# Hybrid attention and mLSTM layer on one core: a sum of weight tiles by GpSimd, a reload in halves, and later modulation items in the first FFN's up projection

## The chip, the cores and the metric

The kernel runs on one core of one Trainium2 chip. The metric is the device time of one execution, in microseconds. The comparison is by medians of several executions; a profile is one further execution, with the hardware profiler on. The engines are called PE (TensorE, matmuls), DVE (VectorE), ACT (ScalarE), POOL (GpSimd) and SP (SyncE, which here only issues transfers). PEld is TensorE's weight load, which runs beside its matmuls.

## What is computed

One layer for 256 latent and 256 context tokens of width 2048, all in fp32: a SwiGLU FFN, a token mixer (grouped attention beside a bidirectional mLSTM), a second FFN, each behind an RMSNorm with shift, scale and gate made from the condition vectors (adaLN). Cut to what the change touches:

```python
def half_step_ffn(x, mod, i, g, w_up, w_down):
    h = adaln(x, g, mod, i)
    a, b = jnp.split(h @ w_up, 2, axis=-1)
    return x + 0.5 * mod[:, i + 2, None, :] * ((jax.nn.silu(a) * b) @ w_down)

mod_l = (silu_c @ w_mod[l] + b_mod[l]).reshape(B, N_MOD, D_MODEL)      # 9 vectors of 2048
mod_c = (silu_cc @ w_mod[l] + b_mod[l]).reshape(1, N_MOD, D_MODEL)
xl = half_step_ffn(xl, mod_l, 0, g_norm[l, 0], w_ffn1_up[l], w_ffn1_down[l])
xc = half_step_ffn(xc, mod_c, 0, g_norm[l, 0], w_ffn1_up[l], w_ffn1_down[l])
hl = adaln(xl, g_norm[l, 1], mod_l, 3)                                 # the mixer: vectors 3 to 5
```

D_FF is 5632, so `w_up` is 2048 x 11264. The products `h @ w_up` are made of 128x512 matmuls in a split form: each fp32 factor is a sum hi + lo of two numbers of a shorter format, and a product is hi*hi + hi*lo + lo*hi, three matmuls (`mm3`, L124 to L126).

## The kernel before

**The stages.** The modulation vectors that the first norm needs come first; then the first FFN's up projection, its down projection, the mixer (from about 1400 us in the profile), and the second FFN (from about 2000 us). Modulation vectors 2 to 8 aren't made on PE: they are dot products on DVE that run beside the other stages as a side job.

**The up projection** takes the 44 column tiles of D_FF in 11 groups of four. The first group goes the plain way. The other ten, n = 1 to 10, are done by `quad(n)`, L660 on: a 2x2 block product with seven products in place of eight. Each quad has seven steps, and each step multiplies one form of the tokens with one form of the weights: `a11`, `a12`, `n1`, `s4`, `s2`, `s3`, `a22` (in the program's names, `hhi` holds the `a` forms and `s3`; `n1h`, `s4h`, `s2h` the others). A step has two weight tiles of 128x2048, q = 0 and 1, so a quad has 14 tiles, each with 24 matmuls of 128x512 (the two halves of the tokens, four blocks of 128 columns, three matmuls each).

**A weight tile** goes through `split` (L90): in two halves of 1024 columns, ACT writes `hi` (L102) and DVE writes `lo` = tile - hi (L103). There are four half buffers of each. PE uses the first half at once and the second six matmuls later.

**Where the tiles come from.** A quad's weights lie in memory as parts (ab, c) of 128x2048, 1 MB each. `chain_[q]` are two tiles in SBUF that hold a running sum. `raw` is a pool of three tiles. In a quad, for each q:

| step | form | tile | issued behind the tile's split |
|---|---|---|---|
| 0 | a11 | chain = part(0, q) | chain += part(1, q) |
| 1 | a12 | raw, loaded part(0, 2+q) | |
| 2 | n1 | chain | chain += part(1, 2+q) |
| 3 | s4 | `ra[q]`, loaded part(1, 2+q) | ra += part(1, q) |
| 4 | s2 | chain | chain += part(0, 2+q): a sum of four |
| 5 | s3 | `ra[q]` | |
| 6 | a22 | chain | reload: the next quad's part(0, q) (`again`, `first_chain`) |

The sums are transfers that add (`accum`, L642), issued on POOL's queue; the loads and the reload are issued by SP. An accumulating transfer waits until ACT and DVE have split the tile that it changes, and the next split of that tile waits until it has landed.

**The modulation items beside it.** `side` (from `mod_items`) does one item at a time: SP loads a 512 KB tile `sraw` (L212, two buffers), and DVE multiplies it with the conditions `cBh` and sums the row, once for each of the two sequences (`scalar_tensor_tensor`, L183). There are 96 items in the ten quads. `cBh` holds half of the conditions and is loaded twice (L178, half 0 and half 1); behind each load the items pause for `WAIT` steps (one step is one weight tile here), and the rest of the pace is a straight line that ends at step (NB - 2) * 14 + 2 = 128. The DVE instructions of the items stay in the order in which the program writes them. Each column of modulation sums that is complete is sent out by `mod_rows_out` two steps later.

`WAIT` (L34) is a global: the mixer's modulation side job (`Beside`, L304) and the second FFN's (`mod_late`, which calls `mod_items`) read it too.

**Order.** Every engine works through its instructions in a fixed order, which a scheduler sets when the program is built, from the order of the code and its own costs; instructions that are pinned (`tc.keep_in_program_order`) keep their order among each other.

Of the kernel before, what the change touches and what calls it, by code (L numbers as in the profile page):

```python
# [11 lines left out]
BF16 = mybir.dt.bfloat16  # L12
AF = mybir.ActivationFunctionType
ALU = mybir.AluOpType
# [16 lines left out]
PACE = 0.5  # L31


WAIT = 2  # L34
BLOCKS = ((0, 2), (2, 4), (4, 8), (8, 12), (12, 16))
FB = 4
CB = 512
# [11 lines left out]
def tile_layer(ctx: ExitStack, tc: tile.TileContext, I: dict, out: bass.AP):  # L49
    nc = tc.nc  # L50
# [124 lines left out]
    def conditions(cB, h0, h1, seqs=(CTX, LAT)):  # L175

        for s in seqs:
            nc.sync.dma_start(cB[s], ccd[s, h0 * 1024 : h1 * 1024].partition_broadcast(P))  # L178

    def mod_half(raw, cB, junk, i, seqs, kt, h):  # L180

        for s in seqs:
            ins = nc.vector.scalar_tensor_tensor(junk() if junk else raw, raw, 1.0, cB[s], op0=ALU.mult, op1=ALU.mult, accum_out=mT[:, i, s, kt, h : h + 1])  # L183
            tc.keep_in_program_order(ins)
# [10 lines left out]
    def mod_items(items, load, raws, n_raws, cB, junk, pace):  # L195

        waits = 0  # L200
        half = None
        done = 0
        late, ahead = [], []

        def step():

            if late and late[0][0] <= done:
                mod_rows_out(*late.pop(0)[1:])

        def fetch(i, kt, h):  # L210
            raw = raws()
            load(raw, I["w_mt"][i - 2, kt, :, h * 1024 : (h + 1) * 1024])  # L212
            ahead.append(raw)

        for item in items[:n_raws]:
            fetch(*item)
        for n, (i, kt, h) in enumerate(items):
            if cB.half(h) != half:
                half = cB.half(h)
                cB.load(half)  # L220
                waits += WAIT
            while done < np.interp(n, *zip((0, 0), *pace)) + waits:
                done += 1
                step()
                yield
            seqs = (CTX, LAT) if i < 5 else (LAT,)
            mod_half(ahead.pop(0), cB.at(h), junk, i, seqs, kt, h)
            if n + n_raws < len(items):
                fetch(*items[n + n_raws])
            left[i] -= 1  # L230
            if not left[i]:
                late += [(done + 2, i, s, v) for s, v in mod_end(i, seqs)]
        while late:
            done += 1
            step()
            yield
# [3 lines left out]
    half_items = lambda i0, i1: [(i, kt, h) for h in range(2) for i in range(i0, i1) for kt in range(KT)]  # L240
# [8 lines left out]
    class Beside:  # L249
# [46 lines left out]
        def steps(self):  # L296
            half = None
            while self.n < len(self.items) or self.due or self.late:
                while self.n < len(self.items):
                    h = self.items[self.n][2]  # L300
                    if h != half:
                        half = h
                        conditions({LAT: self.cB}, h, h + 1, (LAT,))
                        self.waits += WAIT  # L304
                    if self.done < np.interp(self.n, *zip((0, 0), *self.pace)) + self.waits:
# [13 lines left out]
    def mod_end(i, seqs):  # L319

        n, q = divmod(i, 3)
        cols = []
        for s in seqs:
            dst = (SH, SC)[q][:, n, s, :] if q < 2 else sm.tile([P, KT], F32, tag="gv", name="gv")
            mod_sum(dst, i, s, slice(0, KT))
            if q == 1:
                scale_of(n, s, slice(0, KT))
            elif q == 2:
                cols.append((s, dst))
        return cols  # L330

    def mod_rows_out(i, s, v):

        pg = tbank()
        tc.keep_in_program_order(nc.tensor.transpose(pg[:KT, :P], v, ident))
        gr = sm.tile([KT, P], F32, tag="gr", name="gr")
        nc.vector.tensor_copy(gr, pg[:KT, :P])
        nc.sync.dma_start(mod_rows[i][s, :].rearrange("(k p) -> k p", p=P), gr)
# [199 lines left out]
    with pool(name="st", bufs=1) as st:  # L538
# [16 lines left out]
        for k0, k1 in BLOCKS:  # L555
            kk = slice(k0, k1)
            n = (k1 - k0) * P
# [4 lines left out]
            for i in range(2):  # L562
                b = tbank()[:, :n]
                pm.append(b)
                for g in range(KT // nk):
# [6 lines left out]
                    for j in range(nk):  # L572
                        k = nk * g + j
                        q = 32 * (j % 4)
# [31 lines left out]
    NB = NF // FB  # L606
# [5 lines left out]
    def form(tag, name):  # L612
        sp = ft if tag == "t" else fm
        return [sp.tile([P, 2, 8, P], F32R, tag=f"{tag}{x}", name=f"{name}{x}") for x in "hl"]
# [4 lines left out]
    def pinned(ins):  # L619
        tc.keep_in_program_order(ins)  # L620
# [20 lines left out]
    chain_ = [chp.tile([P, 2048], F32, name=f"chain{c}") for c in range(2)]  # L641
    accum = lambda dst, src: nc.gpsimd.dma_start(dst, src, accum_op=ALU.add)  # L642
    with pool(name="f1u", bufs=1) as f1u:
# [14 lines left out]
        def part(n, ab, c):  # L658
            return I["w_up1b"][n - 1, ab, c]

        def first_chain(n, c):
            nc.sync.dma_start(chain_[c], part(n, 0, c))

        for c in range(2):
            first_chain(1, c)
# [13 lines left out]
        n1, s2, s4 = form("n", "n1"), form("s", "s2"), form("t", "s4")  # L679
# [66 lines left out]
        def c12_tile():  # L746
            return f1u.tile([P, CB], F32, tag="c12", name="c12", bufs=2)

        def quad(n, after=lambda step: None):

            X, Y, Z = {}, {}, {}
            ca, cy, cb, ra = {}, {}, {}, {}

            def p1(s):
                ca[s] = ca_tile()
                nc.scalar.activation(ca[s], X[s], AF.Copy)

            def c11(s):
                add(ca[s], Z[s], ca[s])
                nc.scalar.activation(ca[s], ca[s], AF.Silu)  # L760

            def kept(s):
                cy[s] = f1u.tile([P, CB], F32, tag="cy", name="cy", bufs=2)
                nc.scalar.activation(cy[s], Y[s], AF.Copy)

            def p35(s):
                cb[s] = c12_tile()
                nc.scalar.activation(cb[s], Y[s], AF.Copy)

            def c12(s):  # L770
                add(cb[s], X[s], cb[s])
                mul(ca[s], ca[s], cb[s])
                turn.append((n, 2 * s, ca[s]))

            def c22(s):
                add(cy[s], X[s], cy[s])
                ca[s] = ca_tile()
                nc.scalar.activation(ca[s], X[s], AF.Copy)

            def c21(s):  # L780
                add(ca[s], Y[s], ca[s])
                nc.scalar.activation(ca[s], ca[s], AF.Silu)
                mul(ca[s], ca[s], cy[s])
                turn.append((n, 2 * s + 1, ca[s]))

            def chained(ab, c):
                return lambda q: accum(chain_[q], part(n, ab, c + q))

            def again(q):
                if n + 1 < NB:  # L790
                    first_chain(n + 1, q)
                else:
                    nc.sync.dma_start(chain_[q], I["w_dn1"][0, 2 * q])

            def loaded(q):
                ra[q] = raw_tile()
                nc.sync.dma_start(ra[q], part(n, 1, 2 + q))
                return ra[q]

            def plain(q):  # L800
                r = raw_tile()
                nc.sync.dma_start(r, part(n, 0, 2 + q))
                return r

            held = lambda q: chain_[q]
            order = (
                (a11, held, X, True, chained(1, 0), p1),
                (a12, plain, Z, True, None, c11),
                (n1, held, Y, True, chained(1, 2), kept),
                (s4, loaded, Y, False, lambda q: accum(ra[q], part(n, 1, q)), p35),  # L810
                (s2, held, X, False, chained(0, 2), c12),
                (s3, lambda q: ra[q], X, False, None, c22),
                (a22, held, Y, True, again, c21),
            )
            for m, (a, src, dst, fresh, then, use) in enumerate(order):
                if fresh:
                    dst.update({s: bank() for s in range(2)})
                for q in range(2):
                    wt = split(src(q))
                    if then:  # L820
                        then(q)
                    after(2 * m + q)
                    for s in range(2):
                        for j in range(4):
                            k = 4 * q + j
                            hi, lo = a[0][:, s, k, :], a[1][:, s, k, :]
                            mm3(dst[s], hi, lo, *wt(slice(j * CB, (j + 1) * CB)), fresh and k == 0, k == 7, True)
                        if q and use:
                            use(s)
                        elif not s:  # L830
                            turned()

        halves = [cBh[:, q, :] for q in range(2)]
        cond = Conditions(lambda h: h, lambda h: conditions(halves, h, h + 1), lambda h: halves)
        side = mod_items(half_items(2, 5), nc.sync.dma_start, sraw, 2, cond, lambda: c12_tile().bitcast(BF16), ((96, (NB - 2) * 14 + 2),))

        def first_steps(step):
            if step in (1, 2, 3, 4, 5, 6):
# [289 lines left out]
    with ExitStack() as mx:  # L1128
# [288 lines left out]
        for w in range(2):  # L1417
            gs = gains[:, w, :].rearrange("p (a b d) -> p a b d", a=2, b=2)
            for t in range(2):
                nc.vector.tensor_tensor(rt[:, w, t, 0, :], rope[:, t, 0, :], gains[:, w, :], op=ALU.mult)  # L1420
                for b in range(2):
# [4 lines left out]
                        op=ALU.mult,  # L1426
# [262 lines left out]
        for cb in range(NCB):  # L1689
# [3 lines left out]
            c = slice(cb * CB, (cb + 1) * CB)  # L1693
# [187 lines left out]
```

## Time and profile before

| | |
|---|---|
| median of 3 runs | 2715.51 us (2714.76 to 2718.07) |
| the profiled execution | 2715.45 us |
| its span in the trace | 2713.7 us, so 1.75 us lie around it |
| the ten quads | about 164 to 990 us of the span |
| read from memory | 626.31 MB |
| transfers | 104704 packets, 508.98 MB on the hardware queue; 20448 packets, 133.18 MB on POOL's |

How to read the profile. A group's row gives line, engine, operation, out<-in, tile sizes and count, then the busy time and the mean duration in ns, then the time for which the engine was idle just before these instructions and what ended that idle time. A row of the waits gives which engine and line waited for which, the total in us, how many times, and the longest. A row of the timeline gives the start in us, the duration, the engine, the line, the operation, and in brackets the idle time before it. A row of the windows gives the stretch, its length, the busy time of PE, PEld, DVE, ACT and POOL with the numbers of instructions, the granted clock of PE, the busy share of the 16 DMA engines and GB/s. The row of a group of DMA issues gives the count, the KB of each, and the median us from issue to landing. POOLq and SPq are the queues of an engine that issues transfers.

### The profile page before, as it was taken

The page shows a single profiled execution, that of the slowest core. Times are in us where ns is not written, and L with a number is a line of the kernel's source. Part 1 is how long each engine was busy: PE and PEld are TensorE (multiplying, and loading weights), DVE is VectorE, ACT ScalarE, POOL GpSimd, SP SyncE. Part 2 cuts the span into 40 slices and gives each one's busy share as a digit, 9 for nine tenths or more (in the row PEclk, how much of TensorE's full clock was granted, in tenths as well). Part 3 has the DMA queues.
Part 4 walks back from the last instruction along what each step waited for, and adds up shares of the span by engine and source line. Part 5 has one row for each costly group of instructions (what it writes and reads, how often), then busy time and mean ns, then how long its engine had stood idle before and what let it go on. Part 6 is the DMA issues. An engine that isn't in the chain of part 4 may idle for free. (4 is left out here: it accounts for less than half of the span.)

```text
span 2713.7 us, 33046 instructions
## 1 busy us (share of the span) xinstructions
PE 2635.2 (97%) x12573; PEld 2173.0 (80%) x12573; DVE 1993.7 (73%) x2740; ACT 1270.5 (47%) x1592; POOL 177.0 (7%) x223
## 2 busy tenths in 40 slices
PE   6999999999999999999999999999999999999998
PEld 3588878787888778888889888877898888888886
DVE  2387777777878788888886989787675665666557
ACT  3444444444445455444454346355564444444444
POOL 0000001100101000000110000120000000000000
PEclk8999999999999999999999999999999999999999
DMA  8879999998999989888986867574566666666553
GB/s 354 315 231 251 246 271 263 253 277 240 267 261 273 267 235 247 211 219 224 234 244 230 310 229 239 186 250 154 190 233 219 225 226 222 222 227 217 211 196 128
DMA packets 125311, 644.27 MB, mean 237 GB/s; under 512 B 13400, under 2 KB 17496, under 8 KB 67680
## 3 DMA queue, kind: packets, MB, share of 16 engines
q1 hardware_dynamic: 104704, 508.98, 51.8%
q0 software_dynamic: 20448, 133.18, 24.8%
q8 instruction: 99, 1.62, 0.2%
q14 instruction: 60, 0.49, 0.1%
HBM read 626.31 MB, written 15.79 MB: 237 GB/s over the span
## 5 line engine op out<-in xcount | busy, mean ns | idle before, releaser
L103 DVE TENSOR_TENSOR lo<-raw,hi 128x1024 fp32r<-128x1024 f32 (+3 forms) x600 | 720.0, 1206 | 400.0 <-ACT hi L102 385.5
L102 ACT ACTIVATE hi<-raw 128x1024 fp32r<-128x1024 f32 (+3 forms) x600 | 624.6, 1044 | 762.5 <-PE mm L126 628.1
L125 PE MATMUL mm<-lo,hhi 128*128 128x512 f32 (+3 forms) x1024 | 391.3, 382 | 17.0 <-DVE lo L103 16.9
L124 PE MATMUL mm<-hi,hhi 128*128 128x512 f32 (+3 forms) x1024 | 392.1, 386 | 0.0
L126 PE MATMUL mm<-hi,hlo 128*128 128x512 f32 (+3 forms) x1024 | 389.5, 380 | 0.0
L102 ACT ACTIVATE hi<-chain 128x1024 fp32r<-128x1024 f32 x240 | 252.1, 1058 | 266.7 <-PE mm L126 127.0
L103 DVE TENSOR_TENSOR lo<-chain,hi 128x1024 fp32r<-128x1024 f32 x240 | 289.9, 1222 | 104.0 <-ACT hi L102 101.9
L183 DVE SCALAR_TENSOR_TENSOR c<-sraw,cBh 128x1024 bf16<-128x1024 f32 x192 | 229.6, 1220 | 43.0 <-DMA sraw<-in_w_mt 33.2
L124 PE MATMUL mm<-hi,h2hi 128*128 128x512 f32 x640 | 249.3, 390 | 0.0
L126 PE MATMUL mm<-hi,h2lo 128*128 128x512 f32 x640 | 249.2, 389 | 0.0
L125 PE MATMUL mm<-lo,h2hi 128*128 128x512 f32 x640 | 249.2, 389 | 0.0
L125 PEld LDWEIGHTS mm<-lo,hhi 128*128 128x128 f32 x1024 | 194.1, 190 | 54.0 <-DVE lo L103 23.1
L126 PEld LDWEIGHTS mm<-hi,hlo 128*128 128x128 f32 x1024 | 193.8, 189 | 33.6 <-issue 0.2
L124 PEld LDWEIGHTS mm<-hi,hhi 128*128 128x128 f32 x1024 | 193.1, 189 | 31.4
L124 PE MATMUL mm<-hhi,hi 128*128 128x512 f32 (+1 forms) x384 | 142.0, 371 | 1.2 <-ACT hi L102 1.2
L124 PEld LDWEIGHTS mm<-hi,h2hi 128*128 128x128 f32 x640 | 120.2, 188 | 25.1
L126 PEld LDWEIGHTS mm<-hi,h2lo 128*128 128x128 f32 x640 | 120.2, 188 | 24.9
L125 PEld LDWEIGHTS mm<-lo,h2hi 128*128 128x128 f32 x640 | 120.2, 188 | 24.8
L124 PE MATMUL mm<-hi,hid2h 128*128 128x512 f32 x352 | 138.6, 396 | 0.0
L126 PE MATMUL mm<-hhi,lo 128*128 128x512 f32 (+1 forms) x384 | 137.6, 360 | 1.0 <-DVE lo L103 1.0
L125 PE MATMUL mm<-hlo,hi 128*128 128x512 f32 (+1 forms) x384 | 138.1, 360 | 0.0
L126 PE MATMUL mm<-hi,hid2l 128*128 128x512 f32 x352 | 137.2, 390 | 0.0
(383 smaller groups left out, 4745.7 us busy)
## 6 DMA issues: line engine op xcount, KB each, us to landing
raw<-in_w_up2b SPq DMA_DIRECT2D x80, 1024.0 KB, 4.7
raw<-in_w_dn SPq DMA_DIRECT2D x70, 1024.0 KB, 4.8
sraw<-in_w_mt SPq DMA_DIRECT2D x128, 512.0 KB, 6.4
chain<-in_w_up1b POOLq DMA_DIRECT2D x60, 1024.0 KB, 11.1
raw<-in_w_up1b SPq DMA_DIRECT2D x40, 1024.0 KB, 8.5
sr<-in_w_mt SPq DMA_DIRECT2D x69, 512.0 KB, 5.2
mraw<-in_w_m SPq DMA_DIRECT2D x32, 1024.0 KB, 7.5
chain<-in_w_dn POOLq DMA_DIRECT2D x30, 1024.0 KB, 8.6
```

The source lines that it names most:

```text
L102: nc.scalar.activation(hi, src, AF.Copy)
L103: nc.vector.tensor_tensor(lo, src, hi.bitcast(F32), op=ALU.subtract)
L124: nc.tensor.matmul(out_ap, sh, mh, start=first, stop=False, skip_group_check=skip)
L125: nc.tensor.matmul(out_ap, sh, ml, start=False, stop=False, skip_group_check=skip)
L126: nc.tensor.matmul(out_ap, sl, mh, start=False, stop=last, skip_group_check=skip)
L183: ins = nc.vector.scalar_tensor_tensor(junk() if junk else raw, raw, 1.0, cB[s], op0=ALU.mult, op1=ALU.mult, accum_out=mT[:, i, s, kt, h : ...
```

## The change

Four things change.

1. `WAIT` goes from 2 to 3: behind each load of conditions the modulation items pause for three steps, in all three places that read it.
2. The pace of the first FFN's items ends at step 126 in place of 128.
3. The reload of the chain tiles (and their first load) goes as two transfers of 1024 columns each, in place of one of 2048.
4. Step 2 of a quad no longer issues a sum. In step 3, behind the split of `ra[q]`, which holds part(1, 2+q) at that time, POOL adds `ra[q]` to `chain_[q]` in two instructions of 128x1024, and then the sum ra += part(1, q) is issued as before. The sum of four of step 4 and everything else is as it was. Both adds are pinned, on the engine that issues the sums.

```diff
-WAIT = 2
+WAIT = 3
...
+        HALVES = slice(0, 1024), slice(1024, 2048)
+
         def first_chain(n, c):
-            nc.sync.dma_start(chain_[c], part(n, 0, c))
+            for w in HALVES:
+                nc.sync.dma_start(chain_[c][:, w], part(n, 0, c)[:, w])
...
+            def twice(q):
+
+                for w in HALVES:
+                    pinned(nc.gpsimd.tensor_tensor(chain_[q][:, w], chain_[q][:, w], ra[q][:, w], op=ALU.add))
+                accum(ra[q], part(n, 1, q))
+
             held = lambda q: chain_[q]
             order = (
                 (a11, held, X, True, chained(1, 0), p1),
                 (a12, plain, Z, True, None, c11),
-                (n1, held, Y, True, chained(1, 2), kept),
-                (s4, loaded, Y, False, lambda q: accum(ra[q], part(n, 1, q)), p35),
+                (n1, held, Y, True, None, kept),
+                (s4, loaded, Y, False, twice, p35),
                 (s2, held, X, False, chained(0, 2), c12),
...
-        side = mod_items(half_items(2, 5), nc.sync.dma_start, sraw, 2, cond, lambda: c12_tile().bitcast(BF16), ((96, (NB - 2) * 14 + 2),))
+        side = mod_items(half_items(2, 5), nc.sync.dma_start, sraw, 2, cond, lambda: c12_tile().bitcast(BF16), ((96, (NB - 2) * 14),))
```

## The prediction

> **What bounds the kernel now.** Read first the page's busy times, then its queues, then, for the touched stage (164 to 990 us: the first FFN's up projection, ten "quads" of seven steps), TensorE's groups by line, its waits, windows that show the granted clock, and the timeline around the stalls.
>
> ```profile
> PE 2635.2 (97%) x12573; PEld 2173.0 (80%) x12573; DVE 1993.7 (73%) x2740; ACT 1270.5 (47%) x1592; POOL 177.0 (7%) x223
> ...
> q0 software_dynamic: 20448, 133.18, 24.8%
> ...
> L125 PE MATMUL mm<-lo,hhi 128*128 128x512 f32 x640 | 252.9, 395 | 15.1 <-DVE lo L103 15.1
> L125 PE MATMUL mm<-lo,s4h 128*128 128x512 f32 x160 | 64.0, 400 | 7.1 <-DVE lo L103 7.1
> ...
> PE mm L125 <- DVE lo L103: 22.1, 10, 5.2
> ...
> 394.10:397.50 3.40, 3.40 (x8) 2.75 (x9) 2.90 (x3) 0.00 (x0) 0.00 (x0) 0.50 0.93 289
> 971.00:974.40 3.40, 2.87 (x7) 2.29 (x8) 3.08 (x4) 0.00 (x0) 0.00 (x0) 0.50 0.82 255
> 557.90:561.30 3.40, 3.40 (x15) 2.79 (x16) 3.40 (x5) 0.81 (x1) 0.00 (x0) 1.00 0.79 270
> ```
>
> TensorE is the bound: 97% busy, and the change takes no matmul from it. All that can be won in its own stage is TensorE's idle time there: 22.1 us in ten waits for `lo`, the half tiles that DVE makes. A long stall costs a second time. In the windows, columns are length, busy PE, PEld, DVE, ACT and POOL, granted clock, DMA share and GB/s: the 3.4 us from 394.1 have clock 0.50 and 8 matmuls, those from 557.9 clock 1.00 and 15. There are five such half-speed stretches (394.1, 479.5, 616.0, 940.3, 971.0), each losing 3.4 / 2 = 1.7 us, 8.5 in all. At most 22.1 + 8.5 = 30.6 us are there to win.
>
> The stalls are of two kinds, by the tile that TensorE multiplies with.
>
> ```profile
> 390.52 1.23 DVE L183 SCALAR_TENSOR_TENSOR c<-sraw,cBh 128x1024 bf16<-128x1024 f32 x1 [2.05 <-DMA sraw<-in_w_mt]
> ...
> 392.82 1.22 DVE L103 TENSOR_TENSOR lo<-raw,hi 128x1024 fp32r<-128x1024 f32 x1
> ...
> 394.09 0.80 PE L125 MATMUL mm<-lo,hhi 128*128 128x512 f32 x1 [2.05 <-DVE lo L103]
> ...
> 478.36 0.50 PE L125 MATMUL mm<-lo,hhi 128*128 128x512 f32 x1 [1.90 <-DVE lo L103]
> ...
> 725.71 0.50 PE L125 MATMUL mm<-lo,hhi 128*128 128x512 f32 x1 [0.33 <-DVE lo L103]
> ...
> 606.59 1.23 DVE L183 SCALAR_TENSOR_TENSOR c<-sraw,cBh 128x1024 bf16<-128x1024 f32 x1 [4.37 <-DMA cBh<-ccd]
> ...
> 612.85 1.23 DVE L183 SCALAR_TENSOR_TENSOR c<-sraw,cBh 128x1024 bf16<-128x1024 f32 x1 [5.02 <-DMA cBh<-ccd]
> ...
> 615.27 0.50 PE L125 MATMUL mm<-lo,s4h 128*128 128x512 f32 x1 [4.37 <-DVE lo L103]
> ...
> 935.42 1.23 DVE L183 SCALAR_TENSOR_TENSOR c<-sraw,cBh 128x1024 bf16<-128x1024 f32 x1 [7.80 <-DMA sraw<-in_w_mt]
> 939.00 0.50 PE L125 MATMUL mm<-lo,s4h 128*128 128x512 f32 x1 [2.69 <-DVE lo L103]
> ```
>
> **Kind A**, steps 5 and 6 (`hhi`): DVE waits for a modulation tile's transfer (2.05 us for `sraw` at 390.52), both modulation instructions run, and the `lo` half that TensorE needs stands behind them (392.82, then TensorE 2.05 late). Stalls 15.1 us, clock three stretches, 5.1: **20.2**. **Kind B**, step 3 (`s4h`): at 606.59 and 612.85 DVE waits for the conditions `cBh`, at 935.42 for `sraw`; TensorE is 4.37 and 2.69 late. 7.1 and two stretches, 3.4: **10.5**.
>
> So what bounds these stalls is not DVE's work (64 of 81 us in the window of quad 2, quoted next) but DVE's fixed order behind transfers that land late while the 16 DMA engines are full.
>
> **The change, part by part.**
>
> ```profile
> 246.00:327.00 81.00, 81.00 (x367) 67.01 (x366) 63.92 (x81) 38.22 (x44) 7.04 (x8) 1.00 0.96 265
> 266.00:290.00 24.00, 24.00 (x108) 19.88 (x107) 19.82 (x24) 11.69 (x13) 3.53 (x4) 1.00 0.99 249
> 290.00:302.00 12.00, 12.00 (x55) 9.94 (x54) 5.62 (x6) 5.33 (x6) 1.75 (x2) 1.00 1.03 232
> 1400.00:2000.00 600.00, 584.53 (x3245) 506.30 (x3244) 487.04 (x938) 308.05 (x475) 47.26 (x62) 1.00 0.64 222
> ...
> L178 SPq DMA_DIRECT2D cBh<-ccd x2: 550/978/1407, 588.3 to 588.9; - x2
> ...
> 262.71 0.33 SPq L802 DMA_DIRECT2D raw<-in_w_up1b  x1
> ...
> chain<-in_w_up1b POOLq DMA_DIRECT2D x60, 1024.0 KB, 11.1
> raw<-in_w_up1b POOLq DMA_DIRECT2D x20, 1024.0 KB, 12.0
> ```
>
> *Conditions three steps ahead.* The second half of `cBh` is issued at 588.3 and DVE met its two landings at 606.59 and 612.85, a wait of 4.37 and 5.02. One step is about 81 / 14 = 5.8 us: a step more covers 5.8 of each. In the program's order after, the modulation pair of that step moves from between step 3's two tiles to behind both, as it does in quad 10. Kind B 10.5, about 1 left: **-9.5**.
>
> *One sum of four without its transfer.* Removed: 2 of the 6 chain sums per quad, 20 of the 60 on GpSimd's queue, 1.049 MB each, 21.0 MB. That queue moves 133.18 MB in 24.8% of 2713.7 us, 5.05 us of all 16 engines per MB: 106 us, 10.6 per quad of 81, so a DMA share of 0.96 falls to about 0.83. Every other transfer of the stage lands earlier.
>
> *DVE's order.* Read in the two programs' order of instructions: before, in five quads (3, 5, 6, 8, 10) the last half of step 5's second tile stands behind a whole modulation pair; after, in one (4). Kind A by quads: those five hold 15.1 - 1.90 - 0.33 = 12.9 and two clock stretches, 3.4: 16.3, 3.3 each; quads 2, 4, 7, 9 hold 2.2 + 1.7 = 3.9, 1.0 each. After: 8 x 1.0 + 1 x 3.3 = 11.3. The relieved queues I let take half of it away (none to all: 0 to 11.3): 5.7 left. **-14.5**, ends -9 and -20. Late next is quad 4's half, which keeps the bad order, at up to 3.3.
>
> *Four adds on GpSimd per quad*, 128x1024 each, which no row shows.
>
> ```profile
> L1482 POOL TENSOR_TENSOR gm<-gm,mg x4: 1286/1358/1501, 1793.4 to 1825.1; 128x512 f32<-128x512 f32 x4
> ...
> 1793.39 1.29 POOL L1482 TENSOR_TENSOR gm<-gm,mg 128x512 f32<-128x512 f32 x1 [14.44 <-ACT gm L1481]
> 1793.51 2.25 DVE L103 TENSOR_TENSOR lo<-raw,hi 128x1024 fp32r<-128x1024 f32 x1
> ...
> 273.23 1.22 DVE L103 TENSOR_TENSOR lo<-chain,hi 128x1024 fp32r<-128x1024 f32 x1
> ...
> 278.57 0.39 PE L125 MATMUL mm<-lo,n1h 128*128 128x512 f32 x1
> ```
>
> The nearest row is a product at half the width: 1.29 to 1.50 us, median 1.36 (the first line gives ns). At 1024 the add lies between 1.29 (width costs nothing) and 3.00 (twice the slowest). I take 2.45, somewhat under twice the median, as a part of a short instruction should not grow with its width: 9.8 per quad, with ends 5.2 and 12.0. It matters because GpSimd and DVE shut each other out: the `lo` that started 0.12 after GpSimd's product took 2.25 where others take 1.22, and ended 1.08 after it, as if it began only then. So I charge DVE with the full 9.8, not with four times the row's 1.03 = 4.1. DVE is idle for 24 - 19.82 = 4.2 us in 266 to 290 and 12 - 5.62 = 6.4 in 290 to 302, 10.6 together, and its halves are early: the `lo` of 273.23 ends at 274.45, TensorE takes it at 278.57, 4.1 later. If both idle stretches serve, 9.8 fits and TensorE loses nothing; if only the first does, it loses 9.8 - 4.2 - 4.1 = 1.5 per quad (12.0 - 8.3 = 3.7 at the slow end, which is rival B). Over ten quads 0 to 15, and since both idle stretches lie about step 3, where the adds stand, nearer to 0: **+5**.
>
> [...]
>
> The adds wait for the tile's transfer and for DVE's last subtraction from it, as the `ra` sum did. Queued behind them on GpSimd stand that `ra` sum, the second tile's adds and step 4's sums, so each `ra` sum starts 4.9 later; step 5 waits for it. Rival A prices what follows if it is later still. Step 3's splits no longer stand behind a `chain` transfer, and step 4 now waits for the adds.
>
> *The chain's reload in halves.* SP issues 20 more transfers; the first half can land before the second. A gain at step 0 is counted in kind A, whose group has that step's matmuls too. The cost is between nothing and 20 issues at the 0.33 of SP's at 262.71, 6.6 us. I take **0**: SP makes no tile, and `lo` leads TensorE by 4.1 (above), which hides one more issue; without that lead 0.33 would come on each reload.
>
> *Other stages.* WAIT is also read by the mixer's modulation and the second FFN's: their items come a step later. TensorE idles 600 - 584.53 = 15.5 us in 1400 to 2000; a step is 5.8: between -5 and +5, **0**.
>
> Sum against the execution's own 2715.45 (span 2713.7 and 1.75 around it; the median of the runs is 2715.51, so nothing has to be moved): 2715.45 - 9.5 - 14.5 + 5 = 2696.5, say **2697**.
>
> [...] Here 0.50 follows gaps of 2.05 us (394.09) and 1.90 (478.36); the trace decides. [...]
>
> **The rivals.**
>
> ```profile
> 1863.83:1867.27 3.44, 3.10 (x17) 2.35 (x16) 3.39 (x4) 1.07 (x1) 3.44 (x1) 1.00 0.38 160
> ...
> 1863.83 3.44 POOL L131 TENSOR_SCALAR rstd<-hss 128x4 f32<-128x4 f32 x1 [6.75 <-DVE hss L1435]
> ...
> 1709.60 1.46 POOL L1354 TENSOR_SCALAR_AFFINE_SELECT E<-E 128x256 f32<-128x256 f32 x2 [13.02 <-ACT E L1352]
> ...
> 1710.72 1.42 DVE L103 TENSOR_TENSOR lo<-raw,hi 128x1024 fp32r<-128x1024 f32 x1
> ...
> 285.83 0.87 POOL L642 DMA_DIRECT2D raw<-in_w_up1b  x1 [4.98 <-DVE lo L103]
> ...
> 293.29 1.23 DVE L103 TENSOR_TENSOR lo<-chain,hi 128x1024 fp32r<-128x1024 f32 x1 [2.90 <-ACT hi L102]
> ...
> 303.02 1.07 ACT L102 ACTIVATE hi<-raw 128x1024 fp32r<-128x1024 f32 x1 [3.02 <-PE mm L126]
> ...
> 310.04 1.22 DVE L103 TENSOR_TENSOR lo<-raw,hi 128x1024 fp32r<-128x1024 f32 x1
> ...
> 311.73 0.39 PE L125 MATMUL mm<-lo,hhi 128*128 128x512 f32 x1
> ```
>
> *A, slower: the adds wait for DVE, and step 5's tile comes late.* A GpSimd instruction on 128x4 took 3.44 us at 1863.83, during which DVE was busy for 3.39. If the second tile's adds are kept off likewise until DVE's first gap (2.90 before 293.29, so 290.4), they end at 290.4 + 4.9 = 295.3, and the sum into `ra` is issued there instead of at 285.83, 9.5 later. With 12.0 to landing that is 307.3; ACT split that tile from 303.02: 4.3 late. DVE's last half ends at 310.04 + 1.22 = 311.26, 0.5 before TensorE takes it at 311.73: a stall of 3.8 per quad. Nine quads: 34, and 1.7 of clock in half of them, 8: 2715.45 - 24 + 42 = **2733**. It decides from 24 / 9 = 2.7 per quad. Against it: at 1709.60 two GpSimd instructions took 1.46 together, and the `lo` that started at 1710.72, 0.34 before their end, took 1.42: there GpSimd got in and DVE went on. [...]
>
> *B, no change: the adds give the stalls back.* At 3.00 an add, with only the first idle stretch to hide in, TensorE loses 3.7 per quad (above), in two halves each too short for the clock; in six quads, those without a second gap, 6 x 3.7 = 22 against 24 won: **2714**. For it: the adds stand in step 3, where kind B stood. Against it: the second idle stretch of 6.4.
>
> *C, all stalls go*: 30.6 won, adds hidden, other stages -2: 2715.45 - 32.6 = **2683**. For it: a relief of 10.6 us per quad is more than any wait above. Against: one quad keeps the bad order.
>
> That the change doesn't do what it says (the sums still bound by a transfer) would give the reordering alone, and falls in the forecast's range.
>
> **How the numbers follow.** Forecast 0.58, own range 2686 to 2709 (kind A's -20 and the adds at 0; or kind A's -9 and the adds at +12). C 0.09, B 0.13, A 0.20. The range runs from C's 2682 to 2724, the low end of A (2.7 per quad and five clock stretches: 24 + 8.5 against 24): left out are most of A and a little below C. 0.2% is 5.4 us, about what a measurement of this kernel can tell from no change. Faster: forecast and C, 0.67; same: B, 0.13; slower: A, 0.20.
>
> **What would show it.** `mm<-lo,s4h` idle before from 7.1 to about 1, and no `cBh` wait of DVE in front of a `lo`; `mm<-lo,hhi` from 15.1 to about 4; one or two windows at 0.50 left; DMA share per quad about 0.83; GpSimd adds near 2.45 and `lo` halves beside them longer than 1.22. Wrong if the adds take over 3 us or wait for DVE's gaps, if ACT waits for `raw` at step 5, or if TensorE's new waits stand in step 3.

## The result and the profile after

The changed kernel takes 2737.39 us (median of 6 runs, 2736.95 to 2746.56), the kernel before 2716.11 (6 runs, 2710.35 to 2719.57). The ratio is 1.0088, 95% interval 1.0071 to 1.0106: slower by about 21 us, where the forecast was 2697 and the range ended at 2724. The profiled execution took 2743.55, 6 us over the median, with a span of 2741.8. All but about 1 us of the difference arises in the ten quads: their first sum is issued 0.8 us later (164.98 in place of 164.15), the down projection's first matmul comes 27.9 us later (1014.93 in place of 987.04), and the second FFN's first one 27.9 later (1995.07 in place of 1967.22). In the runs below, one of the twelve executions of run 7 took 13713.83 us; it hardly moves that run's median.

The page of the changed kernel, the lines that answer to those quoted of before:

```profile
PE 2644.4 (96%) x12573; PEld 2176.9 (79%) x12573; DVE 2071.3 (76%) x2740; ACT 1266.0 (46%) x1588; POOL 267.9 (10%) x243
...
q0 software_dynamic: 17568, 112.21, 21.1%
```

GpSimd's queue moved 21 MB less, as the change says. But DVE, with the same 2740 instructions, is busy for 77.6 us more. The groups of TensorE, GpSimd and DVE in the stage (164 to 1010, its last 5 us left out) show where:

```profile
L125 PE MATMUL mm<-lo,hhi 128*128 128x512 f32 x633 | 252.6, 399 | 24.9 <-DVE lo L103 24.9
L125 PE MATMUL mm<-lo,s4h 128*128 128x512 f32 x160 | 65.2, 407 | 12.8 <-DVE lo L103 12.8
...
L811 POOL TENSOR_TENSOR chain<-chain,raw 128x1024 f32<-128x1024 f32 x40 | 106.8, 2759 | 139.7 <-DVE lo L103 139.7
...
L183 DVE SCALAR_TENSOR_TENSOR c<-sraw,cBh 128x1024 bf16<-128x1024 f32 x191 | 263.9, 1406 | 36.8 <-DMA sraw<-in_w_mt 36.5
L103 DVE TENSOR_TENSOR lo<-chain,hi 128x1024 fp32r<-128x1024 f32 x159 | 210.7, 1344 | 39.9 <-ACT hi L102 38.6
L103 DVE TENSOR_TENSOR lo<-raw,hi 128x1024 fp32r<-128x1024 f32 x120 | 171.2, 1448 | 42.3 <-ACT hi L102 40.2
```

Neither kind of stall shrank. `hhi` waits 24.9 us where it waited 15.1, `s4h` 12.8 where it waited 7.1. The 40 adds (L811) take 2.76 us on average. DVE's means rose from 1.22 us (its three groups of before had 1220, 1222 and 1223 ns) to 1.41, 1.34 and 1.45: 191 x 0.186 + 159 x 0.122 + 120 x 0.225 = 82 us by which DVE's instructions took longer, 8.2 per quad.

The timeline of one add beside DVE, in quad 4 (GpSimd, DVE and TensorE asked for separately):

```profile
453.07 5.04 POOL L811 TENSOR_TENSOR chain<-chain,raw 128x1024 f32<-128x1024 f32 x2
...
451.72 1.22 DVE L183 SCALAR_TENSOR_TENSOR c<-sraw,cBh 128x1024 bf16<-128x1024 f32 x1
...
452.86 6.34 DVE L183 SCALAR_TENSOR_TENSOR c<-sraw,cBh 128x1024 bf16<-128x1024 f32 x1
...
459.13 2.35 DVE L103 TENSOR_TENSOR lo<-raw,hi 128x1024 fp32r<-128x1024 f32 x2
...
460.40 0.50 PE L125 MATMUL mm<-lo,s4h 128*128 128x512 f32 x1 [3.09 <-DVE lo L103]
```

The modulation instruction of 452.86 takes 6.34 us where its twin just before took 1.22. It ends at 459.20, 1.1 after the second add: DVE did not get in between the two adds either. The `lo` behind it comes late and TensorE stands for 3.09 us. That is the stall in step 3. The one in step 6 of quad 2:

```profile
316.67 1.22 DVE L183 SCALAR_TENSOR_TENSOR c<-sraw,cBh 128x1024 bf16<-128x1024 f32 x1 [3.68 <-DMA sraw<-in_w_mt]
...
319.57 1.22 DVE L103 TENSOR_TENSOR lo<-chain,hi 128x1024 fp32r<-128x1024 f32 x1
...
320.83 0.79 PE L125 MATMUL mm<-lo,hhi 128*128 128x512 f32 x1 [3.12 <-DVE lo L103]
```

No add runs here. DVE waits 3.68 us for `sraw`, and the first `lo` of step 6 stands behind the modulation pair. Eight of the nine quads from the second on have such a stall in `hhi`, 1.95 to 5.43 us.

In the stage PE's clock is at 0.50 for 37.4 us (seven stretches of about 3.4 us and two of about 6.8), so at most 18.7 lost (a little of it falls into the gaps themselves), where it was 8.5 before. Together: waits for DVE 39.4 (24.9 + 12.8 and 1.7 of transposes) against 22.9, clock 18.7 against 8.5, so about 26.7 more, of the 28.1 by which the two profiled executions differ.

### The profile page after: what moved, and what is told of

It is laid out like the page before. It is cut to its first block, busy times and chain, and to the rows that moved or that the text cites. A ratio compares the mean times of both kernels' runs of the same rounds, so it can differ in the third digit from the quotient of the medians.

```text
span 2741.8 us, 33076 instructions
## 1 busy us (share of the span) xinstructions
PE 2644.4 (96%) x12573; PEld 2176.9 (79%) x12573; DVE 2071.3 (76%) x2740; ACT 1266.0 (46%) x1588; POOL 267.9 (10%) x243
## 5 line engine op out<-in xcount | busy, mean ns | idle before, releaser
L103 DVE TENSOR_TENSOR lo<-raw,hi 128x1024 fp32r<-128x1024 f32 (+3 forms) x600 | 745.2, 1249 | 401.7 <-ACT hi L102 387.2
L103 DVE TENSOR_TENSOR lo<-chain,hi 128x1024 fp32r<-128x1024 f32 x240 | 308.8, 1303 | 65.5 <-ACT hi L102 64.1
L183 DVE SCALAR_TENSOR_TENSOR c<-sraw,cBh 128x1024 bf16<-128x1024 f32 x192 | 265.0, 1405 | 36.8 <-DMA sraw<-in_w_mt 36.5
L125 PEld LDWEIGHTS mm<-lo,h2hi 128*128 128x128 f32 x640 | 120.2, 188 | 24.9
L124 PEld LDWEIGHTS mm<-hi,h2hi 128*128 128x128 f32 x640 | 120.2, 188 | 24.9
```

Source lines behind the costliest of these rows:

```text
L103: nc.vector.tensor_tensor(lo, src, hi.bitcast(F32), op=ALU.subtract)
L124: nc.tensor.matmul(out_ap, sh, mh, start=first, stop=False, skip_group_check=skip)
L125: nc.tensor.matmul(out_ap, sh, ml, start=False, stop=False, skip_group_check=skip)
```

## Experiments

Theory L: the adds cost the time, by shutting DVE out (L1) or by holding up what is queued behind them on GpSimd (L2). Rival O: the new order of the modulation items does. DVE's instructions stand in the same order in the changed kernel and in all the kernels below that keep WAIT 3 and the halves, so that those differ in the adds or the transfers alone; the adds on DVE only put their own instructions in between.

| run | us | ratio to before, 95% |
|---|---|---|
| changed kernel | 2737.39 | 1.0088 (1.0071 to 1.0106) |
| 1 WAIT 3 and the pace only | 2714.01 | 0.9990 (0.9977 to 1.0004) |
| 2 sum by transfer, WAIT 3, halves | 2701.48 | 0.9946 (0.9928 to 0.9965) |
| 3 adds of 128x8 | 2693.17 | 0.9917 (0.9896 to 0.9937) |
| 4 two fills per add | 2692.26 | 0.9913 (0.9892 to 0.9933) |
| 5 three fills per add | 2693.77 | 0.9935 (0.9921 to 0.9949) |
| 6 full adds for the first tile only | 2712.16 | 1.0002 (0.9991 to 1.0012) |
| 7 full adds for the second tile only | 2712.27 | 0.9998 (0.9987 to 1.0010) |
| 8 adds on DVE | 2711.63 | 1.0000 (0.9990 to 1.0010) |
| 9 halves only | 2709.68 | 0.9979 (0.9967 to 0.9991) |
| 10 copies in place of adds | 2697.33 | 0.9937 (0.9920 to 0.9953) |
| 11 as 2, all chain and ra sums in halves | 2696.29 | 0.9941 (0.9923 to 0.9959) |
| 12 as 11, raw loads in halves too | 2700.97 | 0.9950 (0.9934 to 0.9966) |

The kernel before had medians of 2715.41 beside runs 1 to 4, 2713.03 beside 5 to 8, 2715.12 beside 9 to 12.

**1. WAIT and pace alone.**

```diff
-WAIT = 2
+WAIT = 3
...
-((96, (NB - 2) * 14 + 2),)
+((96, (NB - 2) * 14),)
```

> The kernel before with WAIT 3 and the pace's end two steps earlier, nothing else of the change. Two theories of the 21 us by which the change is slower. Theory L (the adds on GpSimd: they shut DVE out, 78 us of longer DVE instructions in the stage, and hold up the ra sums behind them): this kernel has no adds, so it is not slower, 2700 to 2714 us, with the two stalls of s4h (7.1 us) nearly gone. Rival O (the later modulation items put DVE's half tiles in a worse order, whatever GpSimd does): 2725 to 2740 us, with stalls of 2 us and more at the first lo of step 6 in most quads, as the changed kernel has them.

2714.01, just at the upper end of what L has, and no sign of O's loss. Its profile, the groups of TensorE and a stall:

```profile
L125 PE MATMUL mm<-lo,hhi 128*128 128x512 f32 x640 | 253.2, 396 | 15.1 <-DVE lo L103 15.1
L125 PE MATMUL mm<-lo,s4h 128*128 128x512 f32 x160 | 62.4, 390 | 0.3 <-DVE lo L103 0.3
...
394.11 1.23 DVE L183 SCALAR_TENSOR_TENSOR c<-sraw,cBh 128x1024 bf16<-128x1024 f32 x1 [2.03 <-DMA sraw<-in_w_mt]
...
397.01 2.35 DVE L103 TENSOR_TENSOR lo<-chain,hi 128x1024 fp32r<-128x1024 f32 x2
...
398.28 0.50 PE L125 MATMUL mm<-lo,hhi 128*128 128x512 f32 x1 [1.49 <-DVE lo L103]
```

Kind B is gone (0.3 us). Kind A has the 15.1 us it had, one place further on: the late transfer now stands in front of the first `lo` of step 6 (397.01, a chain tile) in place of the last of step 5 (392.82 before, a raw tile). O falls as the cause of the slowdown, but the new order by itself is worth little: by the interval between 6 us faster and 1 us slower. The execution profiled here took 2707.64, 6.4 under the median, so its stalls are those of a good execution of this kernel.

**2. The sum by transfer again.**

```diff
-                (n1, held, Y, True, None, kept),
-                (s4, loaded, Y, False, twice, p35),
+                (n1, held, Y, True, chained(1, 2), kept),
+                (s4, loaded, Y, False, lambda q: accum(ra[q], part(n, 1, q)), p35),
```

> The changed kernel with the sum of step 2 put back as an accumulating transfer, and no adds on GpSimd: WAIT, pace and the reload in halves stay, and DVE's order of instructions is that of the changed kernel. Theory L: 2700 to 2716 us, no slower than before, DVE's mean lo of a chain tile back from 1.30 to 1.22 us. Rival O, or that the halves cost something: 2725 us or more. Against the first run it shows what the halves are worth: within 4 us of it if they cost nothing.

2701.48, the whole computation, and faster than both kernels: WAIT and halves together bring 14 us, so all of the loss, and more, lies in step 3's adds, as they stand in this order of DVE's; no run has the adds in the old order. Against run 1 the halves are 12.5 us better, which was not foreseen (run 9).

**3. Tiny adds.** `w` runs over `(slice(0, 8), slice(1024, 1032))`.

> The changed kernel with its adds cut to 128x8 each: same count, same place in GpSimd's queue, same waits, same order on DVE; most of the sum is left out of the output. Theory L: the adds' length is what costs, so this one shows the relief of the transfers alone: 2690 to 2705 us, no lo over 1.3 us, DMA share per quad near 0.8. If the wait of the adds for the tile and not their length were the cost: 2730 us or more. Rival O: 2725 or more.

2693.17: the same instructions on every engine, the same waits, 44 us faster. The length of the adds costs 44 us, and the relief of the transfers brings 8.3 against run 2. The window of quad 2 (length, busy PE, PEld, DVE, ACT, POOL, clock, DMA share, GB/s) and `hhi`:

```profile
247.00:327.00 80.00, 80.00 (x362) 66.17 (x361) 65.60 (x85) 38.45 (x44) 6.99 (x10) 1.00 0.83 232
...
L125 PE MATMUL mm<-lo,hhi 128*128 128x512 f32 x640 | 251.0, 392 | 5.9 <-DVE lo L103 5.9
```

DMA share 0.83 in place of 0.96, and `hhi` waits 5.9 us in place of 15.1.

**4 and 5. GpSimd busy, but not reading.**

```diff
-                    pinned(nc.gpsimd.tensor_tensor(chain_[q][:, w], chain_[q][:, w], ra[q][:, w], op=ALU.add))
+                    for _ in range(2):
+                        pinned(nc.gpsimd.memset(chain_[q][:, w], 0.5))
```

> The changed kernel with each add replaced by two GpSimd fills of the same 128x1024 of the chain tile: GpSimd is kept busy in the same place and queue but reads no SBUF; the sum is left out of the output and the chain overwritten. It parts theory L in two. L1, DVE is shut out while GpSimd reads: lo and the modulation instructions keep 1.22 us, and the time is near that of the tiny adds, 2690 to 2710 us. L2, the ra sums queued behind the adds start late and bunch with the sums of step 4: the fills hold them up likewise, if two fills take about 2.7 us, and the time stays at 2725 to 2740 us.

> The changed kernel with each add replaced by three GpSimd fills of the same 128x1024 (the sum is left out, the chain overwritten): about 3.1 us, longer than an add's 2.70, where the two fills of the run before took 2.05 and were a little shorter. If it is reading SBUF beside DVE that costs (L1): still 2688 to 2698 us and lo at 1.22. If GpSimd's time in its queue counts from some length between 2.05 and 2.70 on (L2): 2710 us or more.

2692.26 and 2693.77, as with the tiny adds. In the run with three fills (124 us of GpSimd's time, more than the adds' 107) the groups of GpSimd and DVE read:

```profile
L812 POOL MEMSET chain<- 128x1024 f32 x120 | 123.9, 1042 | 130.9 <-DVE lo L103 127.5
...
L183 DVE SCALAR_TENSOR_TENSOR c<-sraw,cBh 128x1024 bf16<-128x1024 f32 x192 | 229.4, 1221 | 10.0 <-DMA sraw<-in_w_mt 9.7
L103 DVE TENSOR_TENSOR lo<-chain,hi 128x1024 fp32r<-128x1024 f32 x170 | 205.9, 1223 | 73.8 <-ACT hi L102 71.0
```

DVE kept its 1.22 us. GpSimd's 124 us in its queue cost nothing here (2693.77, beside 2693.17 in run 3): L2 falls as it was put, L1 stands. What is left of L2 is that a DVE which is late also releases the sums late (see the adds, under why the prediction was wrong). Fills don't wait for `ra`, so some of them ran behind the sums that they stood ahead of in the changed kernel; the part of L2 that is a wait for the tile was in run 3 and cost nothing there.

**6 and 7. One tile's adds at a time.** `w` runs over `HALVES` for one q and over the two slices of run 3 for the other.

> The changed kernel with full adds for the first weight tile (q = 0) of each quad only and 128x8 ones for the second, whose sum is left out. The first tile's adds start while DVE waits for step 2's second tile, the second's in the middle of DVE's run of lo halves in step 3. If the place decides: this run is cheap, 2694 to 2704 us, and the next one dear. If only the length by which DVE is shut out counts: about half of the 44 us, 2710 to 2718 us, for each.

> The changed kernel with full adds for the second weight tile (q = 1) of each quad only and 128x8 ones for the first, whose sum is left out. If the place decides: 2712 to 2735 us, most of the 44 us, with the stalls of s4h (12.8 us in the changed kernel) in this run and not in the one before. If only length counts: 2710 to 2718 us.

19 us over the tiny adds for either: the place doesn't decide. DVE's groups, first the run with the first tile's adds, then that with the second's:

```profile
L183 DVE SCALAR_TENSOR_TENSOR c<-sraw,cBh 128x1024 bf16<-128x1024 f32 x192 | 244.1, 1296 | 25.9 <-DMA sraw<-in_w_mt 25.5
L103 DVE TENSOR_TENSOR lo<-chain,hi 128x1024 fp32r<-128x1024 f32 x164 | 218.2, 1342 | 62.5 <-ACT hi L102 59.9
```

```profile
L183 DVE SCALAR_TENSOR_TENSOR c<-sraw,cBh 128x1024 bf16<-128x1024 f32 x192 | 249.9, 1326 | 24.6 <-DMA sraw<-in_w_mt 24.3
...
L103 DVE TENSOR_TENSOR lo<-raw,hi 128x1024 fp32r<-128x1024 f32 x124 | 169.7, 1384 | 64.0 <-ACT hi L102 60.6
```

192 x 0.076 + 164 x 0.120 = 34 us shut out in the one, 192 x 0.106 + 124 x 0.161 = 40 in the other. Neither has the stalls of `s4h` (the second 0.3 us, the first none): those need both. Both have those of `hhi`, 19.1 and 16.9 us, and both have DVE waiting for `sraw` for about 25 us, where 9.7 were left with the fills: being late in step 3 came back as a wait for a transfer in step 6.

**8. The adds on DVE.** `nc.vector` in place of `nc.gpsimd`.

> The changed kernel with the same adds on DVE in place of GpSimd. DVE gets 40 x 1.22 = 49 us of work in place of being shut out for 78, at the same place of its order, and nothing can push in between two halves. Theory L1 (DVE's time lost in and before step 3 is what costs): between the tiny adds' 2693 and the changed kernel's 2737, in proportion 2693 + 44 x 49 / 78 = 2721 us, less if being late by whole instructions matters. If shutting out is dear beyond its length: 2695 to 2710 us.

2711.63, 18.5 over the tiny adds and below the proportion: 40 x 1.22 = 49 us of real work cost no more than 34 to 40 of being shut out.

**9. Halves alone.** `first_chain` of the change in the kernel before.

> The kernel before with the chain's reload in halves only. The sum by transfer with WAIT 3 and the halves (2701.5) was 12.5 us faster than WAIT 3 alone (2714.0), where the prediction had the halves at nothing. If the halves are worth that by themselves: 2700 to 2706 us here. If they help only in the order that WAIT 3 and the pace bring: 2712 to 2718 us, and the 12.5 belong to the two together.

2709.68, 5.4 us faster, between the two cases. WAIT gives 1.4 alone and the halves 5.4, together 13.9. The remaining 7 is within what the executions of one kernel spread by (the kernel before ran from 2703.02 to 2723.96 beside these runs, run 1 from 2707.23 to 2721.43); whether it is an effect of the two together stays open.

**10. Copies.** `nc.gpsimd.tensor_copy(chain_[q][:, w], ra[q][:, w])` in place of the add.

> The changed kernel with each add replaced by a GpSimd copy of the same 128x1024 of ra into the chain: one SBUF input in place of two (the sum is left out, the chain overwritten). If any read of SBUF by GpSimd shuts out DVE's instructions with two inputs: lo and modulation instructions are longer than 1.22 us again, by about as much in all as the copies last, and the time rises over the fills' 2692 by about 0.5 us for each us of it: 2705 to 2725 us. If only GpSimd's second input does it: 1.22 us and 2690 to 2697 us.

```profile
L811 POOL COPY chain<-raw 128x1024 f32<-128x1024 f32 x40 | 51.9, 1397 | 137.0 <-DVE lo L103 137.0
...
L183 DVE SCALAR_TENSOR_TENSOR c<-sraw,cBh 128x1024 bf16<-128x1024 f32 x192 | 240.9, 1278 | 13.9 <-DMA sraw<-in_w_mt 13.6
```

One tile read was enough: 1.28 us where the fills left 1.22. In all 192 x 0.057 + 168 x 0.040 + 128 x 0.035 = 22 us (the `lo` groups had 1262 and 1258 ns), for 4 us of time, not the 0.5 per us expected: the first 20 us or so were nearly free.

**11 and 12. More in halves.**

```diff
-                return lambda q: accum(chain_[q], part(n, ab, c + q))
+                return lambda q: [accum(chain_[q][:, w], part(n, ab, c + q)[:, w]) for w in HALVES]
```

and the `ra` sums likewise; run 12 also loads the raw tiles so.

> The sum by transfer with WAIT 3 and the reload in halves (2701.5 us, faster than both kernels and with the whole computation), with the accumulating transfers of the up projection in halves as well. If what the halves give is that a first half can be split before the second has landed and its transfer starts before the second is split: 2690 to 2700 us, ACT's wait for chain (28 us) shorter. If twice the issues on GpSimd's queue and smaller transfers cost as much: 2698 to 2708 us.

> The same with the loads of the raw tiles in halves too. Raw tiles are loaded long before their use, so nothing more is to be won from an earlier first half: within 4 us of the run before. If SP's queue is late by the 40 more issues: 3 to 10 us slower than it.

2696.29 is the lowest median with the whole computation, 18.8 us below before and 41 below the changed kernel; its ratio and that of run 2 have overlapping intervals, so a gain over run 2 is not shown. ACT's wait for `chain` did not shorten as expected (32.7 us against 28.0, though in the slowest of the six executions, 2706.21), so why halves help was not shown. Run 12 is 4.7 slower, within the spread of both (2694.51 to 2706.21 and 2697.31 to 2703.85).

## Why the prediction was wrong, step by step

- **Conditions three steps ahead, -9.5**: the mechanism was right and its own stalls went (`s4h` 7.1 to 0.3 in run 1), but run 1 as a whole gained only 1.4 us by the medians. Its profiled execution was 7.8 faster than that of before, near the forecast; a typical one was not.
- **DVE's order, half of kind A**: wrong. I followed one instruction, the last half of step 5, and counted in how many quads a modulation pair stood in front of it. The pair moved behind it, and so in front of step 6's first half, which TensorE needs next. Run 1's profile has the same 15.1 us.
- **The halves, 0**: wrong, between 5.4 (run 9) and 12.5 us (run 2 against run 1) in its favour.
- **The relief of the transfers**: right in mechanism and nearly in size: share 0.83 as said, 8.3 us against the 5.7 forecast.
- These errors cancel, which is luck: without the adds the forecast was 2715.45 - 24 = 2691.5, the tiny adds gave 2693.17.
- **The adds, +5 (0 to 15)**: the step that failed; they cost 44. Their length (2.45 taken, 2.76 measured) and the charge on DVE (9.8 per quad taken, 8.2 measured) were right within a fifth. Wrong was what I set against them: 10.6 us of DVE's idle time and a lead of 4.1, as if a late DVE could cost TensorE only what this room does not hold. The idle time was there: in quad 2 nearly all of it (10.7 us between 266 and 302) is DVE waiting for ACT's `hi`, and in the ten quads these waits fell from 133.5 us in run 3 to 78.8 in the changed kernel. But a late DVE cost time in two ways for which my sum had nothing, and the clock came on top.

First, in step 3 itself an instruction that waits out two adds is late by more than the lead: `s4h` waits 12.8 us, where run 3 has no such wait. Second, the sums by transfer wait until DVE has split their tile. I had written that every other transfer lands earlier; with DVE late, the sums start late and close together. GpSimd's issues in quad 2, and the load of `sraw` that DVE needs in step 6, first in the changed kernel, then in run 3 (with the DVE instruction that uses that tile):

```profile
291.65 0.89 POOL L642 DMA_DIRECT2D raw<-in_w_up1b  x1 [1.75 <-DVE lo L103]
295.96 0.87 POOL L642 DMA_DIRECT2D chain<-in_w_up1b  x1 [3.43 <-DVE lo L103]
298.44 0.89 POOL L642 DMA_DIRECT2D chain<-in_w_up1b  x1 [1.60 <-DVE lo L103]
...
308.38 0.33 SPq L212 DMA_DIRECT2D sraw<-in_w_mt  x1
```

```profile
287.64 0.89 POOL L642 DMA_DIRECT2D raw<-in_w_up1b  x1 [4.59 <-DVE lo L103]
292.40 0.87 POOL L642 DMA_DIRECT2D chain<-in_w_up1b  x1 [3.87 <-DVE lo L103]
298.27 0.89 POOL L642 DMA_DIRECT2D chain<-in_w_up1b  x1 [5.00 <-DVE lo L103]
...
308.22 0.33 SPq L212 DMA_DIRECT2D sraw<-in_w_mt  x1
...
312.74 1.22 DVE L183 SCALAR_TENSOR_TENSOR c<-sraw,cBh 128x1024 bf16<-128x1024 f32 x1
```

The three sums start within 6.8 us in place of 10.6, and the last one lands after 16.1 us in place of 11.0. The load of `sraw` goes out at the same time in both, and DVE is ready for the tile about 4.6 us later in both; but it lands after 8.3 us in the changed kernel (316.67, above), and within 4.5 in run 3. The other seven stalls of step 6 are alike: DVE is ready at the same distance from the load in both kernels (3.5 to 4.6 us), and the load lands after 6.8 to 10.0 us in place of 3.5 to 8.3. Over the ten quads the last sum lands after 15.8 us (median), 10.4 in run 3, 10.0 with the three fills of run 5 and 14.0 with the adds on DVE (run 8). So DVE waits for `sraw` for 36.5 us in the changed kernel, 11.2 in run 3 and 9.7 in run 5, in the same order of instructions, and `hhi` for 24.9 in place of 5.9. Of the 47.6 us by which the profiled executions of the changed kernel and of run 3 differ, 12.8 are the wait of `s4h`, 19.0 that of `hhi`, and up to 15.8 the clock (at most 18.7 lost, where the stage's mean clock in run 3 was 1.00). That the close sums make the loads land late is read from the traces; no run tries it by itself.

The price by the time that DVE lost, over the 2693 of runs 3 to 5 (to about 2 us, as the kernel before differed by 2.4 us from one set of runs to another):

| run | DVE shut out, or at work | time |
|---|---|---|
| 10 copies | 22 us | +4 |
| 6, 7 one tile's adds | 34 and 40 | +19, +19 |
| 8 adds on DVE | 49, its own work | +18.5 |
| changed kernel | 82 | +44 |

So about the first 20 us in the stage were nearly free, not the 106 to 147 that my sum allowed; from there on each cost 0.6 to 1.3 us, part of it by the clock: in the changed kernel nine of the ten stalls of 1.9 us and more have a half-speed stretch.

- **Rival A** named 2733, near the measured time, by another mechanism. It had the adds wait for DVE and step 5's tile come late. DVE waited for the adds, and ACT never waited for an `ra` tile in step 5 (the sum of quad 2 landed at 301.7, its split began at 304.75). With GpSimd busy for longer with fills (run 5, 124 us) nothing was lost: 2693.77.
- **Rival B** was nearest in mechanism, the adds giving the stalls back, at too small a price, 22 us for 44: it set the adds at their slow end into one idle stretch of DVE's. It has the stalls in step 3, without clock; of those 12.8 us were measured, and the rest came in step 6 and by the clock.
- **The charge on DVE** held in the runs: beside adds and copies, which read tiles, its `lo` and modulation instructions took longer (means of 1342 and 1296 ns for `lo` of a chain tile and the modulation in run 6, 1384 and 1326 for `lo` of a raw tile and the modulation in run 7, 1262, 1258 and 1278 in run 10), beside fills, which read none, they did not (1221 to 1224 ns in run 5). I took it into the charge and not into the outcome.

## What to carry to other kernels

Work moved to an idle GpSimd was not free here, where DVE is the second-busiest engine (73% before): 107 us of adds cost DVE 82 us, and the same adds on DVE itself were cheaper (2711.63 against 2737.39). Before counting an engine's idle time as room, ask also which transfers wait for its work: in quad 2 the late DVE started its three sums within 6.8 us in place of 10.6, and a later load, issued on time, landed after 8.3 us in place of 4.5 at most. Of a reordered queue, look at every consumer that the moved instruction now stands in front of, not only at the one that it left.

## What the runs showed of the hardware

Two adds stood back to back on GpSimd twelve times. In ten of them DVE did not get in between: the instruction of 452.86 is recorded 0.21 us ahead of the first add and still ended 1.1 us after the second. In the pair from 352.57 it did: an instruction recorded at 353.54 ended at 356.97, 1.1 after the first add, and the second add took 3.39 us; in the twelfth no such instruction was waiting. So the earlier recorded start did not show here which of the two got in first.

An add took 2.39 us at the shortest and 3.39 at the longest, a copy 1.40 and a fill 1.04 on average, all 128x1024.

In the changed kernel the clock went to half speed at gaps of 1.95 us and more, but not at all of them. Windows of the changed kernel behind a gap of 1.95 and one of 2.88:

```profile
576.32 0.50 PE L125 MATMUL mm<-lo,hhi 128*128 128x512 f32 x1 [1.95 <-DVE lo L103]
...
660.49 0.51 PE L125 MATMUL mm<-lo,hhi 128*128 128x512 f32 x1 [2.88 <-DVE lo L103]
...
576.80:580.20 3.40, 3.40 (x10) 2.63 (x9) 3.40 (x5) 0.86 (x1) 0.00 (x0) 0.50 0.92 299
661.00:664.40 3.40, 3.40 (x18) 2.78 (x18) 3.40 (x5) 1.43 (x3) 0.00 (x0) 1.00 0.72 233
```

Of the ten gaps of 1.9 us and more in the stage, nine had such a stretch behind them or from within them, and the 2.88 was the exception. In the kernel before a stretch at 0.50 follows the gap of 1.90 (478.36) and none the one of 1.97 (644.63; 1.00 from 644.6 to 648.0). What decides, the traces don't show.
